# Tokens' high and low parts side by side in a fused transformer block: a layout for products of 512 columns

## The chip, the cores and the metric

The kernel runs on one core of a Trainium2 chip. The metric is the device time of one execution in microseconds (us); less is better. Engines: TensorE (PE; PEld is its weight load), VectorE (DVE), ScalarE (ACT), GpSimd (POOL) and the DMA queues of SyncE (SP) and GpSimd.

## The reference

One transformer block on 256 tokens of 1024 features, all in float32. `D` is 1024, `FF` 2816.

```
mod = silu(c) @ w_ada + b_ada;  sh1, sc1, g1, sh2, sc2, g2 = split(mod, 6)
h = x * (1 + sc1) + sh1
proj = h @ w_in        # attention q, k, v; retention q, k, v; gates rg, g_a, g_r
y = (sigmoid(g_a) * (y_a @ w_proj_moba) + sigmoid(g_r) * (y_r @ w_proj_ret)) @ w_out
x = layer_norm(alpha * x + g1 * y)
h = x * (1 + sc2) + sh2
g = h @ w_ff_gate;  u = h @ w_ff_up
g_conv = causal convolution of g over 3 tokens, per feature, + bias
x = layer_norm(alpha * x + g2 * ((gelu(g_conv) * u) @ w_ff_down))
```

## The kernel before, in words

**Precision.** TensorE works in `F32R`, a rounded float32. To keep float32's precision each operand is split into a high part (the rounded value, written by ScalarE's copy) and a low part (source minus high part, by VectorE's subtraction). A product of two split operands is the sum of three: high by high, high by low, low by high. Weights are loaded as blocks of 1024 KB into `raw` (4 buffers) by SyncE's queue and split half by half into `whi` and `wlo`, 128x1024, 8 buffers each (lines 1149 and 1163).

**Two ways of writing the three products.** With the weights stationary, tokens are the moving operand and the output is features by 256 tokens. `mm3` (line 98) issues three products of 256 columns. `mm2` (line 103) issues two: the high weight against the tokens' high and low parts at once, 512 columns into a whole bank of PSUM, and the low weight against the high part, 256 columns, added to the bank's first half. The two halves of the bank are added afterwards: ScalarE copies the second half, and one step later VectorE adds the first (`wstat8m`, line 373). For `mm2` the two parts must be in one tile. They are, as two planes: the pair `H` is [128, 2, 2048] and `Ya`, `Yb` are [128, 2, 1024], plane 0 high, plane 1 low (`slot`, line 68). The moving operand of 512 columns is therefore read in two stretches of 256, one from each plane.

**Steps.** The work on TensorE after the first stage is a list of steps, one per half block of weights (`weights`, `weights4`); the loop at line 1195 runs them in order. Step numbers here are the variable `s`. Each step first advances the side work (attention, retention, later the residual: `run_sides`), prepares weights of later halves as far as buffers are free (`prep_to`), runs what earlier steps put off to this one (`put_off(n, fn)`: n steps later), and then issues its own products. Every engine takes its instructions in this order.

- Steps 24 to 31: gate of the mixer (`winGr`, `wstat8m`), tokens in `H`. Steps 36 to 43: retention's projection (`wpr`, `wstat8m`), tokens in `Ya`, `Yb` (`S["yr2"]`).
- Steps 48 to 51: the output projection and the first layer norm. Its result is put into `Ya`, `Yb` again (`S["h2"]`). Steps 52 to 55: the first 512 features of the up projection with tokens as the stationary operand (`xs_group`); they end token-major in `u4` and are transposed into `uT` (both in `H`), the second half of them in step 57.
- Steps 56 to 59: gates of rounds 0 and 1, with `wstat8` (line 344): `mm3`, both halves into one bank, then `gate_done` at once on that bank: two ScalarE scalings, four VectorE operations for the convolution, Gelu, the product with `uT` and the split (`act_in`, line 734).
- From step 60: rounds 2 to 10, `wstat8m` for gate and up, with the down projection of earlier rounds between them. `gate_done_m` works per half on a copy in the slot `gu(r)`.

`one_bank` hands out banks 0 to 3 in turn. A slot is one buffer: a new tile in it waits until every use of the old one is over. The residual side work (from step 56) loads the second layer norm's rows by GpSimd's queue; two of them go into `H`, and so wait for the last use of `uT`.

Of the kernel before, what the change touches and what calls it, by code (L numbers as in the profile page):

```python
# [28 lines left out]
T0_AT, XN, PRIME = 4, 256, 3  # L29
W0, W1, W2 = (4, 5), (6,), (7,)  # L30
PIECES = dict(ada1=[4] + [2] * 3 + [1] * 4, winA=[4] * 2 + [2] * 2 + [1] * 4, winX=[1] * 2)
MERGED = 2
CHUNK = 2
BUSY = 3
SEQ = [(s[0], int(s[1])) for s in
# [17 lines left out]
def _body(nc, a, out, pe, act, dve, sp, cst, wts, big, tmp, ps, dram):  # L53
# [4 lines left out]

    place = {0: ("H", 0), 1: ("H", 1), "3a": ("Ya", 0), "6a": ("Ya", 1), "3b": ("Yb", 0), "6b": ("Yb", 1)}
    pairs = {}

    def reopen(dt, *names):
        for n in names:
            pairs[n] = big.tile([128, 2, 2048 if n == "H" else 1024], dt, tag=f"A{n}", name=f"A{n}")

    def slot(n, shape, dt=F32):
        if n in pairs:
            assert pairs[n].dtype == dt  # L70
            return pairs[n].rearrange("p e (k t) -> p e k t", k=shape[2])
        if n not in place:
            return big.tile(shape, dt, tag=f"A{n}", name=f"A{n}")
        pair, e = place[n]
        assert pairs[pair].dtype == dt
        v = pairs[pair][:, e, :math.prod(shape[1:])]
        return v.rearrange("p (a b) -> p a b", a=shape[1]) if len(shape) == 3 else v

# [24 lines left out]
    def mm2(o, wh, wl, x2, start, stop):  # L103


        if start:
            pe.matmul(o, wh, x2, start=True, stop=False)  # L107
        pe.matmul(o[:, :256], wl, x2[:, 0], start=False, stop=False)  # L108
        if not start:
            pe.matmul(o, wh, x2, start=False, stop=stop)  # L110

# [74 lines left out]
    reopen(F32R, "H")  # L186
    hh = slot(0, [128, 8, 256], F32R)
    hl = slot(1, [128, 8, 256], F32R)
    h1x2 = pairs["H"].rearrange("p e (k t) -> p e k t", k=8)
    pa = [bank(i) for i in range(8)]  # L190

    def h1(j, part):
# [136 lines left out]
    def one_bank():  # L329
        i = bank_i[0]  # L330
        bank_i[0] = (i + 1) % 4
        return bank(i)
# [8 lines left out]
        return get  # L341


    def wstat8(name, u, xh, xl, done, mid=None):
        get = lazy(one_bank)

        def mk(half):
            def mm(hi, lo):
                if half and mid:
                    mid()  # L350
                p = get()
                for k in range(8):
                    mm3(p[:, half * 256:half * 256 + 256], hi[:, k * 128:(k + 1) * 128],
                        lo[:, k * 128:(k + 1) * 128], xh(k), xl(k), k == 0, k == 7)
                if half:
                    done(p)
            return mm
        weights(a[name][u], mk(0), mk(1))

    def wstat4(name, u, xh, xl, done):  # L360
        def mk(half):
            def mm(hi, lo):
# [7 lines left out]
            return mm  # L370
        weights(a[name][u], mk(0), mk(1))

    def wstat8m(name, u, x2, copy, done):


        def mk(half):
            def mm(hi, lo):
                p = one_bank()
                for k in range(8):
                    mm2(p, hi[:, k * 128:(k + 1) * 128], lo[:, k * 128:(k + 1) * 128], x2(k), k == 0, k == 7)  # L380
                t = copy(half)
                act.activation(t, p[:, 256:], AF.Copy)  # L382

                def rest():
                    dve.tensor_tensor(t, p[:, :256], t, OP.add)
                    done(half)
                put_off(1, rest)
            return mm
        weights(a[name][u], mk(0), mk(1))
# [40 lines left out]
    for u in range(4):  # L430
        def gr_copy(half, u=u):
            if u == half == 0:
                S["sig", 1] = slot(12, [128, 8, 256])
            return S["sig", 1][:, 2 * u + half]

        def gr_done(half, u=u):
            v = S["sig", 1][:, 2 * u:2 * u + 2]
            if half:
                put_off(1, lambda: act.activation(v, v, AF.Sigmoid))
        wstat8m("winGr", u, lambda k: h1x2[:, :, k], gr_copy, gr_done)  # L440

    for u in range(2):
        def pm_done(half, p, u=u):
# [3 lines left out]
    for u in range(4):  # L447
        def pr_copy(half, u=u):
            if half == 0:
                S["pr"] = slot(("9a", "9b")[u % 2], [128, 2, 256])  # L450
            return S["pr"][:, half]

        def pr_done(half, u=u):
            if not half:
                return
            if u == 0:
                reopen(F32R, "H")
                S["mh"] = slot(0, [128, 8, 256], F32R)
                S["ml"] = slot(1, [128, 8, 256], F32R)
            v, (g, w, mh, ml) = S["pr"], (t[:, 2 * u:2 * u + 2] for t in  # L460
                                          (S["sig", 1], S["sig", 0], S["mh"], S["ml"]))
            dve.tensor_tensor(v, v, g, OP.mult)
            dve.tensor_tensor(v, v, w, OP.add)
            put_off(1, lambda: act.activation(mh, v, AF.Copy))
            put_off(2, lambda: dve.tensor_tensor(ml, v, f(mh), OP.subtract))
        wstat8m("wpr", u, lambda k: S["yr2"][k // 4][:, :, k % 4], pr_copy, pr_done)


    class Norm:
# [144 lines left out]
        weights4(src, [mk(0, 0), mk(0, 1), mk(1, 0), mk(1, 1)], [range(4)] * 4)  # L614

    def out_start():
        S["h2"] = [slot("Y" + e, [128, 2, 4, 256], F32R) for e in "ab"]
        S["h2h"], S["h2l"] = [[t[:, i] for t in S["h2"]] for i in range(2)]
        GB = S["GB"] = tmp.tile([128, 2, 8], F32, name="GB", bufs=1)
        m = mod[:, 2:4]  # L620
        lncol = consts["lncol"]
        dve.tensor_tensor(GB[:, 0], lncol[:, 0], m[:, 0], OP.mult)
        dve.tensor_tensor(GB[:, 1], lncol[:, 1], m[:, 0], OP.mult)
        dve.tensor_tensor(GB[:, 1], GB[:, 1], m[:, 1], OP.add)
        table(AF.Sqrt)
# [54 lines left out]
             {(0, 1, "mid"): ln1_tok1, (0, 1): lambda p: up_tokens(0, p),  # L680
              (1, 1, "mid"): lambda: up_T(0), (1, 1): lambda p: (up_tokens(1, p), table(AF.Gelu))})

    def gate_done(r):
        def fn(p):
            g = slot(("5", "15")[r % 2], [128, 2, 256])
            pv = p.rearrange("p (i t) -> p i t", i=2)
            convw = consts["convw"]
            w = lambda n, i: convw[:, n, 2 * r + i:2 * r + i + 1]
            for i in range(2):
                act.activation(g[:, i], pv[:, i], AF.Identity, scale=w(2, i), bias=w(3, i))  # L690
            for n in (1, 0):
                for i in range(2):
                    dve.scalar_tensor_tensor(g[:, i, 2 - n:], pv[:, i, :254 + n], w(n, i), g[:, i, 2 - n:],
                                             op0=OP.mult, op1=OP.add)
            act.activation(g, g, AF.Gelu)
            S["gelu", r] = g
            if r < 2:
                act_in(r, S["uT"][:, 2 * r:2 * r + 2].rearrange("p a b -> p (a b)"))
        return fn

    def gu(r):

        if ("gu", r) not in S:
# [3 lines left out]
    def gate_done_m(r):  # L707
        def fn(half):
            g, x = gu(r)[:, half], gu(r)[:, 2 + half]
            convw = consts["convw"]  # L710
            w = lambda n: convw[:, n, 2 * r + half:2 * r + half + 1]
            dve.tensor_scalar(g, x, w(2), w(3), op0=OP.mult, op1=OP.add)
            for n in (1, 0):
                dve.scalar_tensor_tensor(g[:, 2 - n:], x[:, :254 + n], w(n), g[:, 2 - n:],
                                         op0=OP.mult, op1=OP.add)
            if half:
                put_off(1, lambda: act.activation(gu(r)[:, :2], gu(r)[:, :2], AF.Gelu))
        return fn

    def up_done_m(r):  # L720
        def fn(half):
# [8 lines left out]
    def a_slots(r):  # L730
        return (slot(("9a", "9b", "10a", "8a")[r % 4], [128, 2, 256], F32R),
                slot(("2a", "2b", "4", "8b")[r % 4], [128, 2, 256], F32R))

    def act_in(r, u):
        g = S.pop(("gelu", r)).rearrange("p a b -> p (a b)")
        dve.tensor_tensor(g, u, g, OP.mult)
        ah, al = a_slots(r)
        split(ah.rearrange("p a b -> p (a b)"), al.rearrange("p a b -> p (a b)"), g)
        S["a", r] = ah, al

    def up_done(r):
        return lambda p: act_in(r, p)

    def down(r, t, hf, hl_, cs, first, last, p=None):
        ah, al = S["a", r]
# [71 lines left out]
                    pass  # L817
        return fn

    h2 = lambda k: S["h2"][k // 4][:, :, k % 4]  # L820

    def ffn_gate(r):
        if r < MERGED:
            wstat8("wgate", r, gh2, gl2, gate_done(r))
        else:
            wstat8m("wgate", r, h2, lambda half: gu(r)[:, 2 + half], gate_done_m(r))

    def ffn_up(r):
        if r < MERGED:
            wstat8("wup", r - 2, gh2, gl2, up_done(r))  # L830
        else:
            wstat8m("wup", r - 2, h2, lambda half: gu(r)[:, 2 + half], up_done_m(r))

    def first():
        bank_i[0] = 0
        up_T(1)

    wstat8("wgate", 0, gh2, gl2, gate_done(0), first)
    ffn_gate(1)
    for r in range(2, NR):  # L840
        ffn_gate(r)
# [169 lines left out]
    def retention():  # L1011
# [60 lines left out]
            yield  # L1072
            yield
        reopen(F32R, "Ya", "Yb")
        S["yr2"] = [slot("Y" + e, [128, 2, 4, 256], F32R) for e in "ab"]
        yrh, yrl = [[t[:, i] for t in S["yr2"]] for i in range(2)]
        for _ in range(3):
            yield
        for w in range(2):
# [231 lines left out]
```

## Time and profile before

| | |
|---|---|
| median of 3 runs | 431.57 us (431.5 to 848.4) |
| profiled execution | 431.75 us, span 430.0 us |
| granted TensorE clock | 0.995 mean |
| busy | PE 97%, PEld 83%, DVE 87%, ACT 58%, POOL 2% |
| chain that ended last | PE 92%, DMA 4%, DVE 2%, ACT 1% |
| HBM | 104.22 MB read, 245 GB/s over the span |

Busy is the share of the span in which an engine works on at least one instruction. The chain that ended last is followed back from the last instruction, each time to what released it. Products overlap in TensorE's pipeline: the duration of one holds its way through the array, and the distance from one start to the next (the pitch) is what a stream of them costs.

### The profile page before, as it was taken

What the parts mean: (1) busy time and instruction counts of PE and PEld (TensorE: products, weight loads), DVE (VectorE), ACT (ScalarE), POOL (GpSimd) and SP (SyncE); (2) the same over time, 40 slices, a digit from 0 to 9 for tenths busy, and PEclk for the clock granted to TensorE, in tenths of its full rate; (3) what the DMA queues carried; (4) which work ended last, traced back from release to release, by engine and by line L of the source; (5) the groups of instructions that cost most, each with busy time, mean ns of one, the idle gap of its engine ahead of it and who ended that gap; (6) DMA issues with size and microseconds to landing.
All of it is one profiled execution on the core that took longest, in us unless ns stands there. A gap on an engine that the chain in (4) does not pass through costs nothing.

```text
span 430.0 us, 6223 instructions
## 1 busy us (share of the span) xinstructions
PE 417.8 (97%) x2322; PEld 355.9 (83%) x2322; DVE 373.6 (87%) x623; ACT 249.3 (58%) x403; POOL 6.7 (2%) x16
## 2 busy tenths in 40 slices
PE   6999999999999999999999999999999999999993
PEld 3678888877788998998889899888888888888882
DVE  5879799969997999999978887899999888789676
ACT  4566667679784469645543894664555555455400
POOL 0000000100000000000000000100000000000000
PEclk9999999999999999999999999999999999999998
DMA  8999986787468777779863066885765776450001
GB/s 271 413 425 368 354 324 272 291 351 246 155 268 300 289 288 271 306 280 353 268 228 128 1 241 248 308 292 200 300 278 210 286 296 237 188 197 1 2 24 73
DMA packets 19838, 105.68 MB, mean 246 GB/s; under 512 B 2528, under 2 KB 4576, under 8 KB 8928
## 3 DMA queue, kind: packets, MB, share of 16 engines
q1 hardware_dynamic: 18432, 100.29, 62.1%
q0 software_dynamic: 1376, 4.99, 3.4%
q8 instruction: 18, 0.29, 0.3%
q14 instruction: 12, 0.10, 0.1%
HBM read 104.22 MB, written 1.06 MB: 245 GB/s over the span
## 4 chain that ended last, share of the span: by engine, by line
PE 92%; DMA 4%; DVE 2%; ACT 1%; issue 0%; SPq 0%; DVEq 0%
PE P L110 20%; PE P L99 14%; PE P L101 14%; PE P L100 14%; PE P L108 11%; PE P L246 6%; DMA raw<-in_strm 4%; PE P L107 3%; PE P L608 1%; PE P L610 1%; PE P L611 1%; PE P L895 1%; PE P L947 1%; PE P L966 1%; PE P L990 1%; DVE junk L182 1%
## 5 line engine op out<-in xcount | busy, mean ns | idle before, releaser
L1163 DVE TENSOR_TENSOR wlo<-raw,whi 128x1024 fp32r<-128x1024 f32 x118 | 142.2, 1218 | 15.6 <-ACT whi L1149 15.6
L1149 ACT ACTIVATE whi<-raw 128x1024 fp32r<-128x1024 f32 x118 | 122.5, 1056 | 28.5 <-PE P L101 8.1
L110 PE MATMUL P<-AYb,whi 128*128 128x512 f32 x176 | 63.5, 396 | 0.0
L182 DVE CUSTOM_DVE_ANT_0 junk<-raw,srow 128x1024 bf16<-128x1024 f32 (+1 forms) x50 | 58.8, 1176 | 2.2 <-ACT srow L169 1.8
L108 PE MATMUL P<-AYb,wlo 128*128 128x256 f32 x176 | 49.0, 279 | 0.0
L110 PE MATMUL P<-AYa,whi 128*128 128x512 f32 x132 | 48.3, 396 | 0.0
L99 PE MATMUL P<-whi,AH 128*128 128x512 f32 (+1 forms) x120 | 46.5, 388 | 0.0
L101 PE MATMUL P<-whi,AH 128*128 128x512 f32 (+1 forms) x120 | 45.2, 376 | 0.0
L100 PE MATMUL P<-wlo,AH 128*128 128x512 f32 (+1 forms) x120 | 45.0, 375 | 0.0
L108 PE MATMUL P<-AYa,wlo 128*128 128x256 f32 x176 | 41.9, 279 | 0.0
L110 PEld LDWEIGHTS P<-AYb,whi 128*128 128x128 f32 x176 | 33.0, 188 | 7.9
L382 ACT ACTIVATE A<-P 128x256 f32<-128x256 f32 x44 | 16.6, 378 | 35.9 <-PE P L110 33.9
L108 PEld LDWEIGHTS P<-AYa,wlo 128*128 128x128 f32 x176 | 33.2, 188 | 3.8
L246 PE MATMUL P<-whi,AH 128*128 128x512 f32 x128 | 33.8, 394 | 1.4 <-ACT AH L210 1.2
L108 PEld LDWEIGHTS P<-AYb,wlo 128*128 128x128 f32 x176 | 33.2, 188 | 0.0
L85 DVE TENSOR_TENSOR wlo<-raw,whi 128x1024 fp32r<-128x1024 f32 (+1 forms) x24 | 24.5, 1045 | 8.2 <-ACT whi L84 8.2
L246 PEld LDWEIGHTS P<-whi,AH 128*128 128x128 f32 x128 | 23.6, 188 | 8.5 <-ACT AH L210 2.5
L84 ACT ACTIVATE whi<-raw 128x1024 fp32r<-128x1024 f32 (+1 forms) x24 | 21.5, 913 | 13.7 <-DMA raw<-in_strm 13.0
L110 PEld LDWEIGHTS P<-AYa,whi 128*128 128x128 f32 x132 | 24.8, 188 | 4.0
L99 PEld LDWEIGHTS P<-whi,AH 128*128 128x128 f32 x120 | 22.6, 188 | 4.9 <-issue 1.3
L101 PEld LDWEIGHTS P<-whi,AH 128*128 128x128 f32 x120 | 22.6, 188 | 4.3
L100 PEld LDWEIGHTS P<-wlo,AH 128*128 128x128 f32 x120 | 22.6, 189 | 3.7
(275 smaller groups left out, 851.8 us busy)
## 6 DMA issues: line engine op xcount, KB each, us to landing
raw<-in_ada SPq DMA_DIRECT2D x16, 1024.0 KB, 5.2
raw<-in_wup SPq DMA_DIRECT2D x11, 1024.0 KB, 5.4
raw<-in_wgate SPq DMA_DIRECT2D x11, 1024.0 KB, 4.8
raw<-in_wdown SPq DMA_DIRECT2D x11, 1024.0 KB, 4.9
raw<-in_winB SPq DMA_DIRECT2D x10, 1024.0 KB, 5.9
raw<-in_strm SPq DMA_DIRECT2D x8, 1024.0 KB, 7.1
raw<-in_strm SPq DMA_DIRECT2D x10, 512.0 KB, 7.2
raw<-in_winGr SPq DMA_DIRECT2D x4, 1024.0 KB, 6.0
```

Of the source, the lines that this page charges most:

```text
L84: act.activation(hi, src, AF.Copy)
L85: dve.tensor_tensor(lo, src, f(hi), OP.subtract)
L99: pe.matmul(o, lh, rh, start=start, stop=False)
L100: pe.matmul(o, lh, rl, start=False, stop=False)
L101: pe.matmul(o, ll, rh, start=False, stop=stop)
L108: pe.matmul(o[:, :256], wl, x2[:, 0], start=False, stop=False)
L110: pe.matmul(o, wh, x2, start=False, stop=stop)
L182: dve.tensor_tensor_reduce(out=junk[:, rows], in0=raw[:, rows], in1=srow[:, rows], scale=1.0, scalar=0.0, op0=OP.mult, op1=OP.add, accum_o ...
L246: pe.matmul(pa[half * 4 + c // 512 * 2 + t], x[:, j, t * 128:(t + 1) * 128], ws[half][k][:, c:c + 512], start=ks == 2 and k == 0 and (j == ...
L382: act.activation(t, p[:, 256:], AF.Copy)
L1149: act.activation(hi, src, AF.Copy)
L1163: dve.tensor_tensor(lo, src, f(hi), OP.subtract)
```

## The change

The tile of a pair becomes [128, k, 512]: for each k-tile the 256 tokens' high parts and, beside them, the 256 low parts. A product of 512 columns reads one stretch. The high and the low part alone are read and written as runs of 256 with a step of 512. Pairs that hold plain float32 keep their two planes. The gates of rounds 0 and 1 are issued with `wstat8m` as the others; `wstat8`, `gate_done`, `act_in` and `MERGED` go. Their convolution is `gate_done_m`; the product with `uT` and the split become `up_old`, written into `uT` in place and put off by further steps. The first gate takes its banks from number 2 on.

```
     def reopen(dt, *names):
         for n in names:
-            pairs[n] = big.tile([128, 2, 2048 if n == "H" else 1024], dt, tag=f"A{n}", name=f"A{n}")
+            w = 2048 if n == "H" else 1024
+            pairs[n] = big.tile([128, w // 256, 512] if dt == F32R else [128, 2, w], dt, tag=f"A{n}", name=f"A{n}")

     def slot(n, shape, dt=F32):
...
+        if dt == F32R:
+            return pairs[pair][:, :, e * 256:e * 256 + 256]
...
-        pe.matmul(o[:, :256], wl, x2[:, 0], start=False, stop=False)
+        pe.matmul(o[:, :256], wl, x2[:, :256], start=False, stop=False)
...
-    def wstat8(name, u, xh, xl, done, mid=None):
-        get = lazy(one_bank)
-        ...
-    def wstat8m(name, u, x2, copy, done):
+    def wstat8m(name, u, x2, copy, done, mid=None):
         def mk(half):
             def mm(hi, lo):
+                if mid:
+                    mid(half)
                 p = one_bank()
...
-        wstat8m("winGr", u, lambda k: h1x2[:, :, k], gr_copy, gr_done)
+        wstat8m("winGr", u, lambda k: h1x2[:, k], gr_copy, gr_done)
...
             if half:
                 put_off(1, lambda: act.activation(gu(r)[:, :2], gu(r)[:, :2], AF.Gelu))
+                if r < 2:
+                    up_old(r)
         return fn
+
+    def up_old(r):
+        def fn():
+            g = S["uT"][:, 2 * r:2 * r + 2]
+            dve.tensor_tensor(g, g, gu(r)[:, :2], OP.mult)
+            ah, al = S["a", r] = a_slots(r)
+            put_off(1, lambda: act.activation(ah, g, AF.Copy))
+            put_off(2, lambda: dve.tensor_tensor(al, g, f(ah), OP.subtract))
+        put_off(2, fn)
...
+    def ffn_gate(r, mid=None):
+        wstat8m("wgate", r, h2, lambda half: gu(r)[:, 2 + half], gate_done_m(r), mid)
...
+    def first(half):
+        if half:
+            up_T(1)
         else:
+            bank_i[0] = 2
+
+    ffn_gate(0, first)
     ffn_gate(1)
```

## Rows read from the trace of the kernel before

**Rows 1.** The page, part 1: busy time, share, number of instructions.

```profile
PE 417.8 (97%) x2322; PEld 355.9 (83%) x2322; DVE 373.6 (87%) x623; ACT 249.3 (58%) x403; POOL 6.7 (2%) x16
```

**Rows 2.** Waits of TensorE, whole span: us in total, times, longest.

```profile
PE P L167 <- DVE sc L160: 3.1, 1, 3.1
PE P L246 <- ACT AH L210: 1.2, 2, 0.8
```

**Rows 3.** Stretches: length, busy us per engine (instructions), granted clock, DMA, GB/s.

```profile
249.54:261.47 11.93, 11.93 (x101) 11.93 (x100) 9.64 (x12) 9.26 (x14) 0.00 (x0) 1.00 0.86 317
261.47:272.65 11.18, 11.18 (x66) 9.75 (x65) 8.51 (x12) 7.83 (x12) 2.08 (x4) 1.00 0.55 185
272.65:283.54 10.89, 10.89 (x50) 9.01 (x48) 10.19 (x17) 5.97 (x10) 0.00 (x0) 1.00 0.98 370
```

**Rows 4.** TensorE's groups by shape, whole span: busy us, mean ns of one.

```profile
L110 PE MATMUL P<-AYb,whi 128*128 128x512 f32 x176 | 63.5, 396 | 0.0
L108 PE MATMUL P<-AYb,wlo 128*128 128x256 f32 x176 | 49.0, 279 | 0.0
...
L108 PE MATMUL P<-AYa,wlo 128*128 128x256 f32 x176 | 41.9, 279 | 0.0
...
L107 PE MATMUL P<-AYa,whi 128*128 128x512 f32 x44 | 17.4, 395 | 0.0
L108 PE MATMUL P<-AH,wlo 128*128 128x256 f32 x64 | 16.6, 279 | 0.0
...
L99 PE MATMUL P<-whi,A9a 128*128 128x512 f32 x22 | 8.6, 389 | 0.0
...
L99 PE MATMUL P<-AYb,whi 128*128 128x256 f32 x16 | 4.5, 283 | 0.0
```

**Rows 5.** TensorE in order of time: start us, duration us, instruction, number.

```profile
249.54 0.27 PE L99 MATMUL P<-AYa,whi 128*128 128x256 f32 x1
...
252.40 0.60 PE L676 MATMUL P<-first,AH 128*128 128x128 f32 x4
252.76 0.36 PE L99 MATMUL P<-AYa,whi 128*128 128x256 f32 x1
...
261.47 0.40 PE L107 MATMUL P<-AYa,whi 128*128 128x512 f32 x1
...
264.52 0.39 PE L108 MATMUL P<-AYa,wlo 128*128 128x256 f32 x2
264.75 0.40 PE L110 MATMUL P<-AYa,whi 128*128 128x512 f32 x1
```

**Rows 6.** VectorE in order of time; in brackets its idle time before, and releaser.

```profile
253.05 5.76 DVE L1163 TENSOR_TENSOR wlo<-raw,whi 128x1024 fp32r<-128x1024 f32 x5 [1.53 <-ACT whi L1149]
258.74 1.64 DVE L693 SCALAR_TENSOR_TENSOR A<-P,convw,A 128x255 f32<-128x255 f32 x4
261.14 0.69 DVE L736 TENSOR_TENSOR A<-AH,A 128x512 f32<-128x512 f32 x1 [0.76 <-ACT A L695]
262.53 0.69 DVE L85 TENSOR_TENSOR A2a<-A,A9a 128x512 fp32r<-128x512 f32 x1 [0.70 <-ACT A9a L84]
...
272.86 0.42 DVE L385 TENSOR_TENSOR A<-P,A 128x256 f32<-128x256 f32 x1
...
273.76 1.00 DVE L714 SCALAR_TENSOR_TENSOR A<-A,convw 128x255 f32<-128x255 f32 x2
274.68 1.22 DVE L1163 TENSOR_TENSOR wlo<-raw,whi 128x1024 fp32r<-128x1024 f32 x1
...
282.97 0.69 DVE L1106 TENSOR_TENSOR A<-A,AH 128x512 f32<-128x512 f32 x1
```

**Rows 7.** ScalarE in order of time: five copies of weights.

```profile
251.98 4.83 ACT L1149 ACTIVATE whi<-raw 128x1024 fp32r<-128x1024 f32 x5
```

**Rows 8.** GpSimd in order of time, and DMA issues (KB each, us to landing).

```profile
269.14 1.05 POOL L1097 DMA_DIRECT2D AH<-in_lnrow x2 [66.81 <-DVE A L736]
...
AH<-in_lnrow POOLq DMA_DIRECT2D x2, 512.0 KB, 4.7
```

More of the change, by code (lines that the diff above doesn't have):

```diff
@@ L31 @@
 PIECES = dict(ada1=[4] + [2] * 3 + [1] * 4, winA=[4] * 2 + [2] * 2 + [1] * 4, winX=[1] * 2)
-MERGED = 2
 CHUNK = 2
@@ L65, in reopen @@
         for n in names:
-            pairs[n] = big.tile([128, 2, 2048 if n == "H" else 1024], dt, tag=f"A{n}", name=f"A{n}")
+            w = 2048 if n == "H" else 1024
+            pairs[n] = big.tile([128, w // 256, 512] if dt == F32R else [128, 2, w], dt, tag=f"A{n}", name=f"A{n}")
     def slot(n, shape, dt=F32):
         if n in pairs:
-            assert pairs[n].dtype == dt
-            return pairs[n].rearrange("p e (k t) -> p e k t", k=shape[2])
+            assert pairs[n].dtype == dt == F32R
+            return pairs[n]
         if n not in place:
@@ L188, in _body @@
     hl = slot(1, [128, 8, 256], F32R)
-    h1x2 = pairs["H"].rearrange("p e (k t) -> p e k t", k=8)
+    h1x2 = slot("H", [128, 8, 512], F32R)
     pa = [bank(i) for i in range(8)]
@@ L341, in lazy @@
         return get
-    def wstat8(name, u, xh, xl, done, mid=None):
-        get = lazy(one_bank)
[L347 to L358, printed above, removed]
     def wstat4(name, u, xh, xl, done):
@@ L465, in pr_done @@
             put_off(2, lambda: dve.tensor_tensor(ml, v, f(mh), OP.subtract))
-        wstat8m("wpr", u, lambda k: S["yr2"][k // 4][:, :, k % 4], pr_copy, pr_done)
+        wstat8m("wpr", u, lambda k: S["yr2"][k // 4][:, k % 4], pr_copy, pr_done)
     class Norm:
@@ L616, in out_start @@
     def out_start():
-        S["h2"] = [slot("Y" + e, [128, 2, 4, 256], F32R) for e in "ab"]
-        S["h2h"], S["h2l"] = [[t[:, i] for t in S["h2"]] for i in range(2)]
+        S["h2"] = [slot("Y" + e, [128, 4, 512], F32R) for e in "ab"]
+        S["h2h"], S["h2l"] = [[slot(n + e, [128, 4, 256], F32R) for e in "ab"] for n in "36"]
         GB = S["GB"] = tmp.tile([128, 2, 8], F32, name="GB", bufs=1)
@@ L681, in _body @@
               (1, 1, "mid"): lambda: up_T(0), (1, 1): lambda p: (up_tokens(1, p), table(AF.Gelu))})
[L683 to L699, printed above, removed]
     def gu(r):
@@ L732, in a_slots @@
                 slot(("2a", "2b", "4", "8b")[r % 4], [128, 2, 256], F32R))
[L734 to L742, printed above, removed]
     def down(r, t, hf, hl_, cs, first, last, p=None):
@@ L818, in tok1, with ffn_up @@
         return fn
[L820 to L824, printed above, removed]
-        else:
[L826 to L838, printed above, removed]
+    h2 = lambda k: S["h2"][k // 4][:, k % 4]
+    def ffn_gate(r, mid=None):
+        wstat8m("wgate", r, h2, lambda half: gu(r)[:, 2 + half], gate_done_m(r), mid)
+    def ffn_up(r):
+        wstat8m("wup", r - 2, h2, lambda half: gu(r)[:, 2 + half], up_done_m(r))
+    def first(half):
+        if half:
+            up_T(1)
+        else:
+            bank_i[0] = 2
+    ffn_gate(0, first)
     ffn_gate(1)
@@ L1074, in retention @@
         reopen(F32R, "Ya", "Yb")
-        S["yr2"] = [slot("Y" + e, [128, 2, 4, 256], F32R) for e in "ab"]
-        yrh, yrl = [[t[:, i] for t in S["yr2"]] for i in range(2)]
+        S["yr2"] = [slot("Y" + e, [128, 4, 512], F32R) for e in "ab"]
+        yrh, yrl = [[slot(n + e, [128, 4, 256], F32R) for e in "ab"] for n in "36"]
         for _ in range(3):
```

## The prediction

> **What bounds the kernel now.** I read the page's engine shares first: TensorE is busy in 417.8 of 430.0 us, VectorE in 373.6 [rows 1]. A busy TensorE can still be waiting, so the waits of TensorE come next: in the whole execution it waits 3.1 us for VectorE and 1.2 us for ScalarE, all at the start of the program [rows 2]. From there to its last product nothing ends a wait on TensorE. What an edit is worth is therefore read from the pitch of products, start to start, and not from any engine's busy share. The table by stretches gives the pitch of three kinds of work at granted clock 1.00 [rows 3]: 32 k-tiles of pairs (a product of 512 columns in two stretches and one of 256) take 11.18 us, 349.4 ns a pair; 48 products of 512 columns in one stretch (two of the 50 counted belong to the neighbours) take 10.89 us, 226.9 ns each. The 96 products of 256 columns of the two gates take 252.40-249.54 and 261.47-252.76, together 11.57 us, 120.5 ns each [rows 5].
>
> **The layout, priced.** The pair must be split into its two products. In the groups that keep shapes apart, 512 columns in one stretch show a mean of 389 ns, in two stretches 396 and 395; 256 columns show 283 ns among their like and 279 ns in a pair [rows 4]. For the two forms whose pitch is known the mean stands 162 ns above it (389 against 226.9, 283 against 120.5), so I read the other two as pitches of 233.5 and 116.5 ns, and they add up to 350, the pair's 349.4. A second sign: two products of 256 columns that follow each other in a pair sequence start at 264.52 and the next of 512 at 264.75, 115 ns each [rows 5]. The 395 ns belong to the product that opens a bank, which follows one of 512; so what comes ahead is not the cause, and the second stretch is the one difference left. Price of the second stretch: at most 349.4-116-226.9 = 6.5 ns; 2.5 ns if the 256-column product goes back to 120; at least nothing, if the excess has another cause. A loss has no row for it: one stretch of 512 is what the down products read. I take 6.5, since both forms' means say it.
> There are 176+176+64 = 416 pairs now [rows 4], in the gates of the mixer, the projection, and rounds 2 to 10. 416 x 6.5 ns = **2.70 us**, all on TensorE and so on the path (0 to 2.70).
>
> **The gates of rounds 0 and 1.** 96 products of 256 become 32 pairs: the columns stay, 32 instructions go. 11.57 us become 32 x 342.9 ns = 10.97, a gain of **0.60 us** (0.39 if a pair stays at 349.4).
>
> **Sum.** 3.30 us off the profiled execution's 431.75 (span 430.0 and 1.75 around it) gives 428.45; that execution is 0.18 above the median of 431.57, so 428.3.
>
> **What the sum costs at nothing, and its cover.** The evacuation of the two gates changes engine and time. Before, VectorE works on the bank at once: four operations in 1.64 us a round, then it waits 0.76 us for Gelu and 0.70 us for the high part [rows 6]. After, each half takes an addition, a scaling and two more, 272.86 to 274.68 = 1.82 us [rows 6], so 3.64 us a round, and the waits go, since Gelu, product and split are put off by steps. So 2.0 us more work a round against 1.46 us of waits. The cover is the lead of prepared weights. What is late next is a bank: the eight halves of steps 56 to 63 take banks 2, 3, 0, 1 twice, so step 63 must find step 59's addition done. VectorE runs five weight subtractions from 253.05 to 258.74, 1.14 us each; then a step costs it 1.82 and a subtraction (274.68), together 2.95. Step 59's addition starts at 258.74+3x2.95+0.6 (round 0's product) = 268.2 and ends at 268.6. TensorE comes to step 63 at 249.54+0.36 (transposes)+7x2.743 = 269.1. The cover is 0.5 us; beyond it each microsecond is paid in full.
> On ScalarE two copies replace two scalings from the same bank, and Gelu waits behind nothing new but for the order: the copy of step 60 must wait until round 0's product has freed slot 5, at 268.8; behind it stand weight copies of 0.97 us [rows 7] for tiles that TensorE wants eight steps later.
> One wait is new on GpSimd's queue. The loads of the layer norm's rows into the H pair are released by the last read of the token-major up products; that is now round 1's subtraction in step 64, about 281, where the trace has the release at 269.14 [rows 8]. Landing takes 4.7 us [rows 8], so the rows arrive near 286.5, and VectorE stands at the residual's first product from 283 [rows 6]: some 3.5 us, with the weight subtractions queued behind. The halves are prepared some 10 us ahead there (the subtraction of 274.68 is for a half used after 283.54), which hides it; with that cover gone it costs 3.5 us.
> The interleaved writes keep their runs of 128 or 256 elements; only the merged split goes from one run of 512 to two, eight operations in all: nothing, at most 0.1 us.
>
> **A rule against the layout.** The rows give two pitches for one column count, 226.9 and 233.5. The Trainium skill, "TensorE: Matmul & The Clock Gate", section "Back-to-back issue gap", lets the gap hang on the column count alone, N/2.4+2.5 ns when warm, so that both layouts cost the same; its 215.8 ns for 512 columns is under both rows here. By that rule the layout term is 0.
>
> **Rivals.**
> *The layout is neutral.* The excess comes from the alternation of 512 and 256 and stays; only the fewer products count, 0.39 us: 431.2. For it: every two-stretch row lies in an alternating stream. Against it: the opening products' 395 ns.
> *Half of it.* The stretch goes, but the 256-column product goes back to 120 ns as in the gates: 416x2.5 ns = 1.04 and 11.57-32x0.3469 = 0.47, so 1.51 us: 430.1. For it: the whole streams' pitches alone say that.
> *Slower: VectorE paces TensorE through steps 58 to 63.* If the order of ScalarE's queue turns each weight copy into a wait of VectorE, four steps lose 0.97 us each, 3.9 us; beyond the cover of 0.5 TensorE waits 3.4 at the banks and the gain of 3.3 is gone: 431.7, and 434.5 with a neutral layout as well. It decides once step 59's addition ends after 269.1. For it: ScalarE was VectorE's releaser in both rounds [rows 6]. Against it: the copies are issued a step ahead and need only banks already finished.
>
> **Chances.** The forecast 0.58 (428.3, own range 427.7 to 428.9), neutral 0.16, half 0.14, VectorE's pace 0.08, anything else 0.04. The range from 427.7 to 431.4 takes in the first three with the bounds of the stretch, and leaves out the slower rival. A difference of 2% (8.6 us) is what a measurement of this kernel surely tells from no change; no case but the last comes near: faster 0.02, same 0.95, slower 0.03.
>
> **What would show it.** Right: 448 pairs of which the 512-column product has a mean near 389 ns, pairs at 343 ns, the stretch of rounds 2 and its like some 0.2 us shorter per 32 pairs; TensorE still without waits after the start; GpSimd's row loads near 280 and a VectorE wait of 3 to 4 us behind them that TensorE does not feel. Wrong: means that stay at 395, a 256-column mean that rises to 283, or a TensorE wait for VectorE between 260 and 272.

## The result, and the profile after

The change makes the kernel slower by a little: 434.52 us median (433.92 to 435.09) against 431.65, ratio 1.0071, 95% interval 1.0058 to 1.0084. One of the four executions of the kernel before took 848.4 us and is left out of the ratio. The forecast was 428.3, its range 427.7 to 431.4. The profiled execution took 433.92 us, span 432.1, that is 2.1 us more of span than before (432.1-430.0).

Page, part 1, of the kernel after: VectorE is busy 2.9 us more than in [rows 1], TensorE 0.5 us more, with 32 instructions fewer.

```profile
PE 418.3 (97%) x2290; PEld 354.3 (82%) x2290; DVE 376.5 (87%) x631; ACT 247.0 (57%) x403; POOL 6.7 (2%) x16
```

The waits of TensorE after (us in total, times, longest) are where the difference begins to show: [rows 2] had two lines, and neither named a down product. L104 is the third product of a triple, the one with the low part of the activations (`al`); L700 is the subtraction that makes this low part, in `up_old`.

```profile
PE P L170 <- DVE sc L163: 3.2, 1, 3.2
PE P L104 <- DVE A2a L700: 1.8, 1, 1.8
PE P L249 <- ACT AH L213: 0.6, 2, 0.4
PE P L104 <- DVE A2b L700: 0.4, 1, 0.4
```

TensorE's groups by shape after (busy us, mean ns): one stretch in place of two, and the 512-column products of pairs still show 396 ns, the 256-column ones 279, as in [rows 4].

```profile
L113 PE MATMUL P<-AYb,whi 128*128 128x512 f32 x192 | 69.3, 396 | 0.0
L111 PE MATMUL P<-AYb,wlo 128*128 128x256 f32 x192 | 53.5, 279 | 0.0
...
L110 PE MATMUL P<-AYa,whi 128*128 128x512 f32 x48 | 19.0, 396 | 0.0
```

TensorE in order of time after, at the first two down steps (64 and 66): start, duration, instruction, in brackets the wait before.

```profile
271.92 0.40 PE L102 MATMUL P<-whi,A9a 128*128 128x512 f32 x1
272.15 0.39 PE L103 MATMUL P<-wlo,A9a 128*128 128x512 f32 x1
274.38 0.50 PE L104 MATMUL P<-whi,A2a 128*128 128x512 f32 x1 [1.84 <-DVE A2a L700]
...
279.73 0.39 PE L103 MATMUL P<-wlo,A9b 128*128 128x512 f32 x1
280.56 0.50 PE L104 MATMUL P<-whi,A2b 128*128 128x512 f32 x1 [0.44 <-DVE A2b L700]
```

The triples from 271.92 to the next pair at 285.70 take 13.78 us; the same 48 took 10.89 before [rows 3]: 2.89 us lost. The start distances hold 2.00 of it at the first wait (2.23 instead of 0.23) and 0.60 at the second; the rest is in the products behind each. Steps 56 to 63 take 271.92-249.06 = 22.86 us against 272.65-249.54 = 23.11 [rows 3, 5]: 0.25 gained. The first gate begins 0.48 us earlier in this execution than in that of before. -0.48-0.25+2.89 is 2.16, the difference of the spans.

VectorE after, in order of time, around the late operations:

```profile
252.58 5.77 DVE L1132 TENSOR_TENSOR wlo<-raw,whi 128x1024 fp32r<-128x1024 f32 x5 [1.53 <-ACT whi L1118]
258.26 0.42 DVE L374 TENSOR_TENSOR A<-P,A 128x256 f32<-128x256 f32 x1
...
267.13 0.68 DVE L697 TENSOR_TENSOR AH<-AH,A 128x512 f32<-128x512 f32 x1
267.74 0.42 DVE L374 TENSOR_TENSOR A<-P,A 128x256 f32<-128x256 f32 x1
...
273.65 0.68 DVE L700 TENSOR_TENSOR A2a<-AH,A9a 128x512 fp32r<-128x512 f32 x1
...
279.82 0.69 DVE L700 TENSOR_TENSOR A2b<-AH,A9b 128x512 fp32r<-128x512 f32 x1
...
287.43 0.69 DVE L1075 TENSOR_TENSOR A<-A,AH 128x512 f32<-128x512 f32 x1 [4.74 <-DMA AH<-in_lnrow]
```

Round 0's low part is begun at 273.65, where before it was begun at 262.53 [rows 6]: eleven us later, and 1.7 us after TensorE began the step that wants it (271.92). VectorE shows no wait between 252.58 and 277.8; the operation simply stands that far back in the queue.

### The profile page after: what moved, and what is told of

Same layout as the page of the kernel before. It is cut to its first block, busy times and chain, and to the rows that moved or that the text cites. A ratio compares the mean times of both kernels' runs of the same rounds, so it can differ in the third digit from the quotient of the medians.

```text
span 432.1 us, 6165 instructions
## 1 busy us (share of the span) xinstructions
PE 418.3 (97%) x2290; PEld 354.3 (82%) x2290; DVE 376.5 (87%) x631; ACT 247.0 (57%) x403; POOL 6.7 (2%) x16
## 4 chain that ended last, share of the span: by engine, by line
PE 83%; DVE 7%; DMA 4%; ACT 3%; issue 2%; SPq 0%; DVEq 0%
PE P L113 18%; PE P L102 13%; PE P L104 13%; PE P L103 13%; PE P L111 10%; PE P L249 6%; DMA raw<-in_strm 4%; PE P L110 3%; DVE wlo L1132 2%; ACT whi L1118 1%; DVE A L685 1%; PE P L864 1%; PE P L916 1%; PE P L935 1%; PE P L959 1%
## 5 line engine op out<-in xcount | busy, mean ns | idle before, releaser
L113 PE MATMUL P<-AYb,whi 128*128 128x512 f32 x192 | 69.3, 396 | 0.0
L111 PE MATMUL P<-AYb,wlo 128*128 128x256 f32 x192 | 53.5, 279 | 0.0
L113 PE MATMUL P<-AYa,whi 128*128 128x512 f32 x144 | 52.8, 396 | 0.0
L111 PE MATMUL P<-AYa,wlo 128*128 128x256 f32 x192 | 45.7, 279 | 0.0
L104 PE MATMUL P<-whi,AH 128*128 128x512 f32 (+1 forms) x120 | 45.2, 376 | 0.0
L113 PEld LDWEIGHTS P<-AYb,whi 128*128 128x128 f32 x192 | 36.0, 188 | 8.7
L111 PEld LDWEIGHTS P<-AYa,wlo 128*128 128x128 f32 x192 | 36.2, 189 | 4.1
L371 ACT ACTIVATE A<-P 128x256 f32<-128x256 f32 x48 | 18.1, 377 | 33.4 <-PE P L113 19.8
L111 PEld LDWEIGHTS P<-AYb,wlo 128*128 128x128 f32 x192 | 36.2, 188 | 0.0
L113 PEld LDWEIGHTS P<-AYa,whi 128*128 128x128 f32 x144 | 27.0, 188 | 4.3
L104 PEld LDWEIGHTS P<-whi,AH 128*128 128x128 f32 x120 | 22.6, 188 | 4.3
```

Of the source, the lines that this page charges most:

```text
L104: pe.matmul(o, ll, rh, start=False, stop=stop)
L111: pe.matmul(o[:, :256], wl, x2[:, :256], start=False, stop=False)
```

## The experiments

Theories: A, the loss is the late low part of rounds 0 and 1, late through its place in VectorE's queue, and the layout is neutral; B, the interleaved layout costs time somewhere; C, VectorE's added work in rounds 0 and 1 is paid in whatever order it stands.

**The layout alone** (before, with the pairs as [128, k, 512], gates as they were):

```
-        pe.matmul(o[:, :256], wl, x2[:, 0], start=False, stop=False)
+        pe.matmul(o[:, :256], wl, x2[:, :256], start=False, stop=False)
...        # reopen, slot and the views of the pairs as in the change
```

> The kernel before with the new layout of the pairs alone; the gates of rounds 0 and 1 stay with three products of 256 columns and their old evacuation. Theory A (the loss is the late low part of rounds 0 and 1, which comes with the gates' new evacuation; the layout is neutral): ratio to before 0.999 to 1.001, 512-column products of pairs keep a mean of 395 to 396 ns, no wait of TensorE after the start. Theory B (interleaved high and low parts cost time somewhere): ratio near 1.006.

431.53 us against 431.49, ratio 1.000 (0.9991 to 1.0008); TensorE does not wait after the start, and with one stretch the products of 512 columns keep the mean that they had with two:

```profile
L113 PE MATMUL P<-AYb,whi 128*128 128x512 f32 x176 | 63.5, 396 | 0.0
```

The layout neither costs nor brings anything: theory B is out, and with it the prediction's largest term.

**The gates alone** (the change with two planes put back: the diff above, reversed):

> The change with the two-plane layout put back: only the gates of rounds 0 and 1 as pairs, with their new evacuation. Theory A: ratio 1.005 to 1.008 as the whole change, with TensorE waiting about 2 us for the subtraction of round 0's low part in the first down step. Theory B: ratio 0.999, no such wait.

434.40 us against 431.49, ratio 1.0070 (1.0058 to 1.0082). The whole loss comes with the gates; the waits are the same two:

```profile
PE P L101 <- DVE A2a L697: 1.9, 1, 1.9
...
PE P L101 <- DVE A2b L697: 0.4, 1, 0.4
```

**Product and split one step earlier** (the change with one number altered):

```
             put_off(2, lambda: dve.tensor_tensor(al, g, f(ah), OP.subtract))
-        put_off(2, fn)
+        put_off(1, fn)
```

> The change with one number altered: product and split of rounds 0 and 1 are put off by one step fewer. Theory A: the low part of round 0 is ready at about 270.5 us, before TensorE's first down step at 272; both waits of TensorE go, 431.2 us, ratio 0.999, and run to run the time is as steady as before (within 0.3 us). Theory B: ratio stays near 1.006. A third, theory C (VectorE's 2 us of added work a round are what is paid, in whatever order): ratio stays above 1.003.

431.95 us against 431.49, ratio 1.0014 (1.0005 to 1.0022). Most of the loss is gone, not all. The wait for round 0 is gone; the one for round 1 stayed:

```profile
PE P L104 <- DVE A2b L700: 0.5, 1, 0.5
```

VectorE in this kernel, in order of time. The profiled execution is the slowest of the eleven (433.09 us), and its first gate begins 1.1 us later than after the change, so times are counted from the first gate's first product (250.19 us here, 249.06 after the change): round 0's subtraction comes 3.0 us earlier and round 1's 2.0, since nearly the same work still stands ahead of them.

```profile
271.80 0.69 DVE L700 TENSOR_TENSOR A2a<-AH,A9a 128x512 fp32r<-128x512 f32 x1
...
278.92 0.68 DVE L700 TENSOR_TENSOR A2b<-AH,A9b 128x512 fp32r<-128x512 f32 x1
```

My expectation that both waits go was wrong, and so was the one of a steady time (within 0.3 us): the eleven executions took 431.58 to 433.09. What a step number buys depends on the queue's backlog, the work that still stands ahead in it. Part of C was still open.

**The low part one step later** (one execution):

```
-            put_off(2, lambda: dve.tensor_tensor(al, g, f(ah), OP.subtract))
+            put_off(3, lambda: dve.tensor_tensor(al, g, f(ah), OP.subtract))
```

> The change with the low part alone put off by one step more. Theory A: round 0's subtraction moves behind one more weight subtraction and one more evacuation, to an end near 278 us; TensorE's wait for it grows from 1.8 to 5 to 6 us and the time to about 437. Theories B and C: no change, 434.

439.22 us, where 437 was expected. The wait grew to 5.4 us, as A says; B and C are out as sole causes. But the time grew by 2 us more than the waits did (439.22-433.92 = 5.3 against 5.4-2.3 = 3.1). TensorE in order of time, and then the stretches of this execution (length, busy us per engine, granted clock, DMA share, GB/s):

```profile
278.05 0.79 PE L104 MATMUL P<-whi,A2a 128*128 128x512 f32 x1 [5.41 <-DVE A2a L700]
278.64 0.63 PE L102 MATMUL P<-whi,A9a 128*128 128x512 f32 x1
279.06 0.63 PE L103 MATMUL P<-wlo,A9a 128*128 128x512 f32 x1
...
282.48 0.63 PE L102 MATMUL P<-whi,A9a 128*128 128x512 f32 x1
282.90 0.52 PE L103 MATMUL P<-wlo,A9a 128*128 128x512 f32 x1
```

```profile
262.00:272.00 10.00, 10.00 (x59) 8.71 (x58) 9.64 (x18) 5.45 (x9) 0.00 (x0) 1.00 0.60 211
272.00:285.00 13.00, 7.59 (x23) 5.74 (x22) 9.54 (x16) 5.39 (x8) 0.00 (x0) 0.74 0.43 161
285.00:300.00 15.00, 15.00 (x80) 12.82 (x79) 9.87 (x15) 6.26 (x9) 2.10 (x4) 1.00 0.83 278
```

From 278.64 to 282.90 ten products take 426 ns each instead of 227: TensorE runs at its lower level of 1.2 GHz after standing still for 5.4 us. That costs 10 x 0.2 = 2.0 us on top of the wait.

**The same work, ahead of fewer weights** (the change; from the end of step 55 to step 65 weights are prepared at most four halves ahead instead of eight):

```
-            prep_to(max(need) + 1 + (LOOKAHEAD if s < LN1_AT - 1 else HL_BUFS))
+            ahead = LOOKAHEAD if s < LN1_AT - 1 else 4 if LN1_AT + 8 <= s < LN1_AT + 18 else HL_BUFS
+            prep_to(max(need) + 1 + ahead)
...
-                prep_to(max(need) + 1 + HL_BUFS)
+                prep_to(max(need) + 1 + (4 if s == LN1_AT + 7 else HL_BUFS))
```

> The change with weights prepared at most four halves ahead from the end of step 55 to step 65, so that three weight subtractions leave VectorE's queue ahead of the evacuation of rounds 0 and 1; its work is the same. If what is paid is the place in the queue (theory A): the low parts of rounds 0 and 1 end near 271 and 277 us, before TensorE wants them at 272.4 and 277.8; no wait of TensorE after the start, 431.2 us, ratio 0.999 (the gates' own gain of 0.25 us is left). If VectorE's added work is paid in whatever order (theory C): ratio stays at 1.003 or more.

431.20 us against 431.56, ratio 0.9993 (0.9984 to 1.0002). VectorE carries out the same operations, two weight subtractions stand ahead of the first evacuation instead of five, and the low parts are in time (TensorE's step 64 begins at 272.09, its step 66 at 277.55):

```profile
252.75 2.36 DVE L1132 TENSOR_TENSOR wlo<-raw,whi 128x1024 fp32r<-128x1024 f32 x2 [1.53 <-ACT whi L1118]
255.03 0.42 DVE L374 TENSOR_TENSOR A<-P,A 128x256 f32<-128x256 f32 x1
...
270.43 0.68 DVE L700 TENSOR_TENSOR A2a<-AH,A9a 128x512 fp32r<-128x512 f32 x1
...
276.05 0.68 DVE L700 TENSOR_TENSOR A2b<-AH,A9b 128x512 fp32r<-128x512 f32 x1
```

TensorE's waits in this kernel, all at the start:

```profile
PE P L170 <- DVE sc L163: 3.1, 1, 3.1
PE P L249 <- ACT AH L213: 0.4, 1, 0.4
```

So the place in the queue is the cause, not the work: C is out. This is the fastest version run, but its interval takes in 1: the gates as pairs are worth 0.36 us at the median here and 0.25 in the trace, which this measurement cannot tell from nothing.

**What makes the 396 ns.** Three experiments on the products by themselves, one execution each. First, the change with the pair's second product widened to 512 columns (this adds the low by low products):

```
-        pe.matmul(o[:, :256], wl, x2[:, :256], start=False, stop=False)
+        pe.matmul(o, wl, x2, start=False, stop=False)
```

> The change with the second product of each pair taken over all 512 columns (the low by low products are added to the second half of the bank, so the output changes by them). No product of 256 columns is left in the pairs. If the neighbourhood of products of 256 columns made the 396 ns: the 512-column products of pairs fall to 389 ns and a pair takes 2 x 226.9 = 453.8 ns. If the tokens as moving operand made them: they stay at 395 to 396 ns and a pair takes 467.

Then the same in the kernel before, which reads two stretches (the output changes in the same way):

```
-        pe.matmul(o[:, :256], wl, x2[:, 0], start=False, stop=False)
+        pe.matmul(o, wl, x2, start=False, stop=False)
```

> The same widening of the second product, made to the kernel before, where each product of 512 columns reads two stretches. If a second stretch costs nothing: 389 ns and 453.8 ns a pair, as with the side by side layout. If it costs the 6.5 ns of the prediction: 396 ns and 467 ns a pair here, and 389 and 453.8 there.

TensorE's groups by shape, the first fence with one stretch, the second with two:

```profile
L113 PE MATMUL P<-AYb,whi 128*128 128x512 f32 x192 | 74.7, 389 | 0.0
L111 PE MATMUL P<-AYb,wlo 128*128 128x512 f32 x192 | 74.7, 389 | 0.0
```

```profile
L108 PE MATMUL P<-AYb,wlo 128*128 128x512 f32 x176 | 68.5, 389 | 0.0
L110 PE MATMUL P<-AYb,whi 128*128 128x512 f32 x176 | 68.5, 389 | 0.0
```

Both have 389 ns. In both, the 64 products of a round's gate and up stages take 14.5 us, 226.7 ns each (one stretch: 303.21 to 317.72; two: 300.63 to 315.13). A second stretch costs nothing, and tokens as the moving operand do not make a product longer than weights do. The two kernels take 478.01 and 475.40 us, since TensorE works on more columns. The first of them also bears on theory A: it has VectorE's order and work of the change, but TensorE gets to the down products later, and it has no wait for the low parts (round 0's is begun at 287.78, its first reader at 292.78). Last, the down projection of rounds 0 to 6 in the kernel before, with its middle product in two of 256 columns:

```
...        # for each bank p: the high by high product of 512 columns
+                    for i in (0, 256):
+                        pe.matmul(p[:, i:i + 256], ah[:, half, tk], lo[:, c + i:c + i + 256], start=False, stop=False)
...        # the low by high product of 512 columns
```

> The kernel before with the middle product of the down projection of rounds 0 to 6 split into two of 256 columns each, which all read one stretch. If a neighbour of 256 columns makes a 512-column product longer in the record: these 512-column products rise from 389 to about 395 ns and the 256-column ones show 279. If not: 389 and 279 to 283.

432.31 us. Its down products, which all read one stretch, now show what only pairs showed before:

```profile
L766 PE MATMUL P<-whi,A2a 128*128 128x512 f32 x16 | 6.3, 396 | 0.0
...
L763 PE MATMUL P<-whi,A9a 128*128 128x512 f32 x16 | 6.3, 395 | 0.0
...
L765 PE MATMUL P<-wlo,A9a 128*128 128x256 f32 x32 | 6.3, 278 | 0.0
```

So the neighbourhood of 256-column products is what shifts both means, the one up and the other down. Whichever way the record shares it out, a pair takes 349.4 ns, 2.5 more than 226.9 and 120. What these 2.5 ns are, no run here shows.

## Why the prediction was wrong

*The layout, -2.70 us: wrong, 0.* I took the difference of two means, 396 against 389, as the price of the second stretch, on the assumption that a mean stands the same 162 ns above its pitch in a mixed stream as among its like. The difference is the mark of a mixed stream. The second sign, 115 ns for each of two products of 256 columns, is there with one stretch as well (255.37 to 255.60 after the change). The argument against the alternation, that the product opening a bank follows one of 512 columns, looked at one neighbour only: the next product has 256 columns there too. The prediction's lower bound, "nothing, if the excess has another cause", was the true end. With this term alone wrong, the time would have stayed inside the range: the neutral rival's 431.2 is what the rationed version takes (431.20). The Trainium skill, "TensorE: Matmul & The Clock Gate", section "Back-to-back issue gap", gives the gap of an isolated product by its number of columns alone. These runs agree in that the layout does not enter it (226.7 ns with one stretch and with two); the fixed 2.5 ns given there is not what they show, 226.9-213.3 = 13.6 ns a product of 512 columns at 2.4 GHz.

*The gates as pairs, -0.60 us: right in sign, 0.25 in the trace* (0.39 was given for pairs that stay at 349.4).

*"The waits go, since Gelu, product and split are put off by steps": the step that failed.* The prediction followed VectorE's queue operation by operation, 2.95 us a step, and the queue came out as worked out: step 59's addition was to start at 268.2 and starts at 267.74, the bank was in time, TensorE did not wait in steps 58 to 63. It even placed round 1's subtraction at about 281 (it began at 279.82). But it set that number only beside GpSimd's row loads, and not beside the down products of step 66, which read this low part at 278; for round 0's low part, read in step 64 at 272, it worked out no time at all. Its sign of being wrong, a wait of TensorE between 260 and 272, therefore ended just ahead of the wait, which began at 272.5. Of an operation that is put off, every reader has to be asked, and TensorE was the nearer one. This is a wait that takes the place of those removed: VectorE's 0.76 and 0.70 us a round, off the path, became 2.00 and 0.60 us of TensorE's, on it (2.89 us with the products behind each).

*The slower rival* had the right pair of engines and the wrong place: banks in steps 58 to 63 instead of the low parts in 64 and 66, and ScalarE's order instead of the backlog of five weight subtractions. That its time with a neutral layout, 434.5 (its terms add up to 434.6), is the time measured is luck.

*The row loads on GpSimd's queue: right, a little small.* The loads were issued at 281.09, as forecast, and took 6.7 us to land instead of 4.7. VectorE stood 4.74 us at the residual (3.5 forecast), and TensorE has no wait behind it: the lead of prepared weights hid it, as said. The rationed version shows 2.2 us there.

*What stays open.* The trace accounts for 2.16 us; the medians differ by 2.9 (434.52-431.65). The traced execution is the shortest of the change's four. With the gates alone and with the change, the executions of 434.8 to 435.2 us show a mean granted clock of 0.991 to 0.992, those of 433.6 to 434.2 us 0.994 to 0.995. A fall like the one behind the 5.4 us wait would fit the longer times, but none of them has a trace: this is argued and not shown.

## What to carry to other kernels

When work is put off to clear an engine's waits, write down for each result the start of its first reader on every engine and the place of the operation in its own queue; a step number says nothing of when a queue with a backlog gets there. Where a lookahead fills that queue with work that is wanted later (here 7 to 14 us), rationing it can do more than moving the urgent operation: 431.20 us here against 431.95 for the step moved. And price a form of product from the pitch of the whole repeating group, never from the mean duration of one member.

## What was not expected of the hardware

- In a stream that mixes products of 512 and 256 columns the record shows 395 to 396 ns for the one and 278 to 279 for the other; among their like they show 389 and 283. The pitch of a pair exceeds the sum of the pure pitches by 2.5 ns only. Whether the moving operand lies in one stretch or in two of 256 does not matter (389 and 389).
- After TensorE had stood still for 5.4 us its products started 426 ns apart, the level of 1.2 GHz, for 4.3 us, which cost 2.0 us; after 1.84 us, in the profiled execution of the change, they started some 230 ns apart, and the granted clock is 1.00 from 272 to 278.
- The mean granted clock of an execution is a weak witness: the profiled one of the version with product and split a step earlier shows 0.946, and its products of 512 columns still start 226.7 ns apart (275.79 to 276.47, three of them).
